# A quarter of a depthwise convolution on GpSimd, and half-array float32 matmuls in turn on both halves of the array

## The chip, the cores and the metric

The kernel runs on one core of one Trainium2 chip. The metric is the time of one execution in microseconds (us), the median of three runs. One execution was profiled; the rows below are from it. The names used are those of the profile: PE is TensorE (matmuls), PEld its weight loads, DVE is VectorE, ACT is ScalarE, POOL is GpSimd, SP is SyncE, which issues most DMAs.

## What is computed

Two model blocks of two layers each, on 256 tokens of width 1024, everything in float32. Two of the token mixers matter here. The first mixer of the first block (the hybrid) contains an attention with a compressed branch: windows of 32 keys (and of 32 values), 15 of them, go through a small network with a gelu. The first mixer of the second block (the even mixer) runs on two streams of 256 tokens (`lat` and `ctx`) and has a convolution branch beside a differential attention.

```
def compress(a, j):                              # hybrid: keys j=0, values j=1
    blocks = a[:, :, blk_idx] + cmp_pe[j]
    h = jax.nn.gelu(blocks.reshape(B, G, n_cmp, CMP_BLOCK * Dh) @ cmp_w1[j])
    return h @ cmp_w2[j]
...
def conformer_conv(p_glu, conv_w, conv_b, ln_g, ln_b):     # even mixer: 512 channels, 31 taps
    a, gate = jnp.split(p_glu, 2, axis=-1)
    u = depthwise_conv(a * jax.nn.sigmoid(gate), conv_w, conv_b)
    return jax.nn.silu(layer_norm(u, ln_g, ln_b))
...
def diff_attend(q, k, v, lam):                   # even mixer
    s = jnp.einsum('bhmqd,bhmkd->bhmqk', q, k).astype(F32) * (DIFF_DQK ** -0.5)
    p = jax.nn.softmax(s, axis=-1)
    p = p[:, :, 0] - lam * p[:, :, 1]
    return jnp.einsum('bhqk,bhkv->bhqv', p.astype(v.dtype), v)
...
    y_lat = jnp.concatenate([conv_lat, diff_merge(o, subln_g, lambda_init)], axis=-1) @ w_out
```

## The kernel before, in words

The kernel is one long program. Each engine executes its own instructions in program order; the order is made by a scheduler from the order of the source and from priorities, so a change in the source can move instructions on an engine. Engines wait for each other by semaphores only.

A projection multiplies the tokens by a weight matrix that streams from memory in tiles of 128x2048 (`wraw`, 1 MB). So that float32 accuracy comes out of a faster matmul form, each half tile (128x1024) is split into a high part `whi` (ACT, L424) and a low part `wlo` (DVE, `wlo = wraw - whi`, L427), and three matmuls replace one (L444 to L446, L506 to L509). Per half tile the DVE thus owes one `wlo`, and PE cannot finish with that half tile before it. The scores, the attention outputs and the compressed branch are plain float32 matmuls; one such matmul stands in the trace as two records.

**The even mixer** (`even_mixer`, from L1889) begins with its projections. The first gives the convolution input, in four groups of 128 channels (j = 0 to 3): `up` holds a group's 2x256 inputs, padded, and `cu[:, j]` its 2x256 outputs. Tap 0 is done on ACT (L1923); each of the other 30 taps is one DVE instruction, `c = u*w + c` over 128x512 (L1933). They are issued in `conv_taps`: all 30 of j = 0, 1 and 2 while the projections run, at a low priority, so that they fill the gaps between the instructions `wlo`. The 30 taps of j = 3 are held in a list and issued in two pieces of 15 after the first and the second attention head. Then come the projections of q and k (`ev_qk`, with a rotation on the DVE, L1943 to L1945) and of v (`ptok`). After the projections follow four attention heads (scores `psc` L1992, row maxima `emx` L1994, softmax, transposes `ppt` L2007, values `poT` L2018). Each head's output is normalised: PE sums squares (`pn`, L617), POOL computes a power of -0.5 (`rir`, L593, 128x4), PE spreads it (`prb`, L629). `conv_norm` takes the channel mean of `cu` (matmul `pmu` L1957) once all taps are done, and has a `rir` of its own. PE fills the gaps of this stage with matmuls for the later adaptive normalisation (`pada` L826), which wait for weights from memory. The output projection ends the mixer.

**The hybrid mixer** (`hybrid`, from L1010) has scores for two groups g of heads, whose keys lie in partitions 0 to 63 (g = 0) and 64 to 127 (g = 1), so each score matmul uses half of the rows of the PE array. The attention outputs (`oT`, L1102) use half of its columns. The compressed branch multiplies 30 rows (2 groups x 15 windows) by `cmp_w1`, 4 tiles of 1 MB that POOL's queue loads: 16 matmuls for j = 0, then 16 for j = 1 (`pc`, L1126), all in the same columns of the array.

Of the kernel before, what the change touches and what calls it, by code (L numbers as in the profile page):

```python
# [8 lines left out]
F32 = mybir.dt.float32  # L9
# [3 lines left out]
OP = mybir.AluOpType  # L13
# [312 lines left out]
TAPJ = (30, 30, 30, 0)  # L326
# [685 lines left out]
def hybrid(S, h, x, gate):  # L1012
    nc, tc, A = S.nc, S.tc, S.A
    mm = nc.tensor.matmul
    with ExitStack() as st:
# [37 lines left out]
        stk = stkb[:, :1024].rearrange("p (j g t) -> p j g t", j=2, g=2)  # L1053
        blk = stkb[:, 1024:1984].rearrange("p (j o g n) -> p j o g n", j=2, o=16, g=2)
        for g in range(2):
            nc.gpsimd.dma_start(stk[0:64, :, g], kk[g * 64:(g + 1) * 64, 0:2])
            nc.gpsimd.dma_start(stk[64:128, :, g, 0:255], kk[g * 64:(g + 1) * 64, 0:2, 1:256])
        pc = S.ps("pc", (128, 2, 256))[:30]
        for j in range(2):
            for g in range(2):  # L1060
                src = bass.AP(tensor=stkb.tensor, offset=stk[:, j, g].offset, ap=[list(stk[:, j, g].ap[0]), [2, 16], [16, 15]])
                nc.vector.tensor_tensor(blk[:, j, :, g], src, pe[:, j * 16:(j + 1) * 16, None].to_broadcast([128, 16, 15]),
                                        op=OP.add)
# [4 lines left out]
        def scores(bi, qt):  # L1068

            kt, n = 2 + bi, 128 * (qt + 1)  # L1070
            sc = big("sc")[:, :8 * n].rearrange("p (i n) -> p i n", i=8)
            for i2 in range(4):
                p = S.ps("psc", (128, 2, 256))
                for a in range(2):
                    i = i2 * 2 + a
                    g, r = i // 4, i % 4
                    b = slice(g * 64, g * 64 + 64)
                    mm(p[:, a, :n], q2[b, r, qt * 128:(qt + 1) * 128], kk[b, kt, :n], start=True, stop=True)
                    nc.vector.scalar_tensor_tensor(sc[:, i], kn(f"d{qt}")[:, :n], slopes[i], p[:, a, :n],
                                                   op0=OP.mult, op1=OP.add)  # L1080
# [24 lines left out]
        def values(bi, qt, sc):  # L1105
            vo = 128 * bi
            for ks in range(qt + 1):
                for g in range(2):
# [18 lines left out]
        u = wk.tile([30, 2, 256], F32, name="gel", tag="e1", bufs=1)  # L1127
        z = wk.tile([30, 2, 256], F32, name="gelz", bufs=1)
        nc.scalar.activation(u, pc, AF.Square)
# [33 lines left out]

        hc = wk.tile([128, 2, 2, 30], F32, name="hc", bufs=1)
        ph = S.ps("phc", (128, 2, 2, 30))
        for j in range(2):
            for hh in range(2):
                nc.tensor.transpose(ph[:, j, hh], z[:, j, hh * 128:(hh + 1) * 128], S.ident[0:30, 0:30])
        nc.vector.tensor_copy(hc, ph)
# [4 lines left out]
        for g in range(2):  # L1174
            for hh in range(2):
                mm(pkc[g * 64:(g + 1) * 64, :15], w2j[:, 0, hh], hc[:, 0, hh, g * 15:(g + 1) * 15], start=hh == 0, stop=hh == 1)
        nc.vector.tensor_copy(kcp[:, :15], pkc[:, :15])
        rep = wk.tile([128, 2, 2, 4, 32], F32, name="rep", bufs=1)
        nc.gpsimd.memset(rep, 0.0)
        for hh in range(2):  # L1180
            for g in range(2):
                nc.vector.tensor_copy(rep[:, hh, g, :, :15], hc[:, 1, hh, None, g * 15:(g + 1) * 15].to_broadcast([128, 4, 15]))
        vcp = []
# [29 lines left out]
        for qt in range(2):  # L1213
            for i in range(8):
                g, r = i // 4, i % 4
# [62 lines left out]
        nc.scalar.activation(pct, pt, AF.Copy)  # L1278
        for g in range(2):
            for r in range(4):  # L1280
                to_o((r, slice(0, 256)), slice(g * 64, g * 64 + 64), vcp[g][:, r], pct[:, g].rearrange("p a b -> p (a b)"))
# [608 lines left out]
def even_mixer(S, hs, xs, gates, neglam, then):  # L1890
# [3 lines left out]
    with ExitStack() as st:  # L1894
# [17 lines left out]
        def ev_conv(f, p):  # L1912
# [66 lines left out]
        def weights_of(hh):  # L1979

            PTs = []
            for i in range(2):
# [3 lines left out]
                for qt in range(2):  # L1986
                    es, rs = [], []
                    for m in range(2):
                        b = slice(m * 64, m * 64 + 64)
                        p = S.ps("psc", (128, nk))  # L1990
                        for a, ks in enumerate(keys):
                            mm(p[:, a * 256:(a + 1) * 256], q[b, hh, i, qt * 128:(qt + 1) * 128], k[b, hh, ks], start=True, stop=True)  # L1992
                        mx = S.sm.tile([128, 1], F32, name=f"emx{m}")
                        nc.vector.tensor_reduce(mx, p, axis=AX, op=OP.max)  # L1994
# [609 lines left out]
```

## Time and profile before

| | |
|---|---|
| median of 3 runs | 2766.69 us (2766.11 to 2767.92) |
| the profiled execution's own time | 2766.61 us |
| its span in the profile | 2764.8 us |
| mean granted TensorE clock | 0.985 of full speed |
| PE busy | 2660.5 us (96%) |
| DVE busy | 1820.6 us (66%) |
| POOL busy | 70.9 us (3%) |

The even mixer's projections and attention lie between about 1585 and 1853 us of the span, the hybrid between 84 and 226 us. The shares of the whole say little on these stretches; the rows further down take them one by one.

### The profile page before, as it was taken

What the parts mean: (1) busy time and instruction counts of PE and PEld (TensorE: products, weight loads), DVE (VectorE), ACT (ScalarE), POOL (GpSimd) and SP (SyncE); (2) the same over time, 40 slices, a digit from 0 to 9 for tenths busy, and PEclk for the clock granted to TensorE, in tenths of its full rate; (3) what the DMA queues carried; (4) which work ended last, traced back from release to release, by engine and by line L of the source; (5) the groups of instructions that cost most, each with busy time, mean ns of one, the idle gap of its engine ahead of it and who ended that gap; (6) DMA issues with size and microseconds to landing.
All of it is one profiled execution on the core that took longest, in us unless ns stands there. A gap on an engine that the chain in (4) does not pass through costs nothing. (4 is left out here: it accounts for less than half of the span.)

```text
span 2764.8 us, 42440 instructions
## 1 busy us (share of the span) xinstructions
PE 2660.5 (96%) x17080; PEld 2135.2 (77%) x17080; DVE 1820.6 (66%) x3010; ACT 1158.5 (42%) x1675; POOL 70.9 (3%) x115
## 2 busy tenths in 40 slices
PE   6999999999899999999999899889999999999999
PEld 2768999879656656555565598489988999799999
DVE  5475888887645555544555487769755467768754
ACT  3354445554644445444444322423222345223543
POOL 0100000000000000000000000000000011000000
PEclk9999999999899999999999999999999999999999
DMA  7645895444799999999999722535555214002552
GB/s 252 226 174 200 339 343 206 181 167 152 295 420 422 413 419 423 404 382 416 408 421 422 319 93 70 205 115 181 197 187 183 92 48 176 30 1 87 205 184 91
DMA packets 92843, 659.95 MB, mean 239 GB/s; under 512 B 10548, under 2 KB 10821, under 8 KB 13982
## 3 DMA queue, kind: packets, MB, share of 16 engines
q1 hardware_dynamic: 89582, 641.62, 59.5%
q0 software_dynamic: 3056, 15.53, 1.6%
q8 instruction: 136, 2.23, 0.3%
q14 instruction: 69, 0.57, 0.1%
HBM read 651.87 MB, written 4.72 MB: 237 GB/s over the span
## 5 line engine op out<-in xcount | busy, mean ns | idle before, releaser
L427 DVE TENSOR_TENSOR wlo<-wraw,whi 128x1024 fp32r<-128x1024 f32 (+1 forms) x683 | 811.0, 1218 | 338.1 <-ACT whi L424 335.3
L424 ACT ACTIVATE whi<-wraw 128x1024 fp32r<-128x1024 f32 (+1 forms) x683 | 705.1, 1054 | 723.4 <-PE oacc L564 182.3
L563 PE MATMUL oacc<-act_h,whi 128*128 128x256 f32 (+1 forms) x720 | 226.9, 316 | 0.0
L564 PE MATMUL oacc<-act_l,whi 128*128 128x256 f32 (+1 forms) x720 | 226.8, 315 | 0.0
L565 PE MATMUL oacc<-act_h,wlo 128*128 128x256 f32 (+1 forms) x720 | 226.8, 315 | 0.0
L792 DVE SCALAR_TENSOR_TENSOR macc<-wraw,srow 128x1024 f32<-128x1024 f32 x144 | 175.9, 1221 | 8.6 <-DMA wraw<-in_ada_dram 4.1
L565 PEld LDWEIGHTS oacc<-act_h,wlo 128*128 128x128 f32 x720 | 135.7, 188 | 10.2
L563 PEld LDWEIGHTS oacc<-act_h,whi 128*128 128x128 f32 x720 | 135.7, 189 | 10.0
L564 PEld LDWEIGHTS oacc<-act_l,whi 128*128 128x128 f32 x720 | 135.6, 188 | 10.0
L507 PE MATMUL pm<-h_lo,whi 128*128 128x256 f32 x512 | 132.7, 280 | 0.0
L506 PE MATMUL pm<-h_hi,whi 128*128 128x256 f32 x512 | 132.1, 278 | 0.0
L427 DVE TENSOR_TENSOR eal<-pat,eah 128x512 fp32r<-128x512 f32 x28 | 19.4, 691 | 167.0 <-ACT eah L424 167.0
L506 PE MATMUL pws<-h_hi,whi 128*128 128x256 f32 x416 | 112.1, 283 | 4.5 <-DVE xg L642 4.5
L1753 PE MATMUL pu<-wraw,gq 128*64 128x512 f32 x448 | 113.4, 595 | 0.0
L507 PE MATMUL pws<-h_lo,whi 128*128 128x256 f32 x416 | 111.4, 282 | 0.0
L1758 ACT ACTIVATE ea<-pg 128x512 f32<-128x512 f32 x42 | 25.1, 597 | 203.8 <-PE pg L1753 162.7
L445 PE MATMUL pyl<-wlo,eah 128*128 128x512 f32 x224 | 90.5, 404 | 18.6 <-DVE wlo L427 17.5
L509 PE MATMUL pm<-h_hi,wlo 128*128 128x256 f32 x512 | 106.8, 279 | 0.0
L444 PE MATMUL pws<-h_hi,whi 128*128 128x256 f32 x352 | 103.5, 294 | 0.0
L1759 DVE TENSOR_TENSOR ea<-ea,pu 128x512 f32<-128x512 f32 x42 | 28.9, 687 | 112.3 <-PE pu L1753 79.6
L1753 PE MATMUL pg<-wraw,gq 128*64 128x512 f32 x448 | 101.3, 595 | 0.0
L446 PE MATMUL pws<-h_hi,wlo 128*128 128x256 f32 x352 | 101.1, 287 | 0.0
(788 smaller groups left out, 6536.0 us busy)
## 6 DMA issues: line engine op xcount, KB each, us to landing
wraw<-in_moe_gu_dram SPq DMA_DIRECT2D x224, 1024.0 KB, 10.0
wraw<-in_moe_down_dram SPq DMA_DIRECT2D x112, 1024.0 KB, 9.6
wraw<-in_mlp_dram SPq DMA_DIRECT2D x64, 1024.0 KB, 4.8
wraw<-in_ada_dram SPq DMA_DIRECT2D x48, 1024.0 KB, 4.8
wraw<-in_dense_gu_dram SPq DMA_DIRECT2D x22, 1024.0 KB, 5.8
wraw<-in_hyb_mod_dram SPq DMA_DIRECT2D x12, 1024.0 KB, 7.1
wraw<-in_dense_mod_dram SPq DMA_DIRECT2D x12, 1024.0 KB, 4.8
wraw<-in_ssm_xbc_dram SPq DMA_DIRECT2D x12, 1024.0 KB, 4.7
```

Of the source, the lines that this page charges most:

```text
L424: self.nc.scalar.activation(hi, src, AF.Copy)
L427: self.nc.vector.tensor_tensor(lo, src, hi, op=OP.subtract)
L444: mm(out, l[0], r[0], start=start, stop=False)
L446: mm(out, l[1], r[0], start=False, stop=stop)
L506: mm(p[:, i], hi[:, k], hs[i][0][:, k], start=st, stop=False, skip_group_check=True)
L507: mm(p[:, i], hi[:, k], hs[i][1][:, k], start=False, stop=False, skip_group_check=True)
L509: mm(p[:, i], lo[:, k], hs[i][0][:, k], start=False, stop=k == 7, skip_group_check=True)
L563: mm(p, wh, h, start=start, stop=False, skip_group_check=True)
L564: mm(p, wh, l, start=False, stop=False, skip_group_check=True)
L565: mm(p, wl, h, start=False, stop=stop, skip_group_check=True)
L792: nc.vector.scalar_tensor_tensor(junk, r[:, j], 1.0, s, op0=OP.mult, op1=OP.mult, accum_out=t[:, f:f + 1])
L1753: mm(pg[gu][q], g[2][:, i, q], w[:, k], start=i == 0, stop=i == 7, skip_group_check=True)
```

## The change

It has two parts, which touch each other nowhere.

The first is in the even mixer. The 30 taps of group j = 3 leave the DVE: POOL does each as two instructions over 128x512, `t = u*w` and `c = c + t`, as soon as that group's `up` and its tap 0 are there, that is during the projections. `t` is a single buffer in SBUF, as are `u` and `c`. The DVE keeps the 90 taps of j = 0 to 2, and the attention stage has no DVE taps any more.

The second concerns matmuls that use half of the array (or fewer columns): in the hybrid's scores, attention outputs and compressed scores and in the even mixer's scores, consecutive matmuls now alternate between the two halves. In the compressed branch, j = 0 and j = 1 go to columns 0 to 31 and 32 to 63 and alternate; the blocks are padded from 30 to 32 columns by a small memset on POOL, the four tiles of `cmp_w1` are loaded in another order (first halves of both j, then second halves), and the gelu runs on 64 partitions x 256 in place of 30 x 512.

```
@@ hybrid
-        blk = stkb[:, 1024:1984].rearrange("p (j o g n) -> p j o g n", j=2, o=16, g=2)
+        blk = stkb[:, 1024:2048].rearrange("p (j o m) -> p j o m", j=2, o=16)
+        nc.gpsimd.memset(blk[:, :, :, 30:32], 0.0)
...
-        pc = S.ps("pc", (128, 2, 256))[:30]
+        pc = S.ps("pc", (128, 256))[:64]
...
-            for i2 in range(4):
-                p = S.ps("psc", (128, 2, 256))
+            for r2 in range(2):
+                ps = [S.ps("psc", (128, 2, 256)) for _ in range(2)]
                 for a in range(2):
...
+                    for g, p in enumerate(ps):
+                        b, r = slice(g * 64, g * 64 + 64), r2 * 2 + a
+                        mm(p[:, a, :n], q2[b, r, qt * 128:(qt + 1) * 128], kk[b, kt, :n], start=True, stop=True)
...
-                    for r in range(4):
+                    both.append(pts)
+                for r in range(4):
+                    for g, pts in enumerate(both):
                         to_o((r, slice(qt * 128, qt * 128 + 128)), slice(g * 64, g * 64 + 64),
...
-        for j in range(2):
-            w1t = [S.raw(A["cmp_w1"][j, :, o * 2048:(o + 1) * 2048], nc.gpsimd).rearrange("p (a b) -> p a b", b=256) for o in range(2)]
-            for o in range(16):
-                mm(pc[:, j], blk[:, j, o].rearrange("p g n -> p (g n)"), w1t[o // 8][:, o % 8], start=o == 0, stop=o == 15)
+        for o2 in range(2):
+            w1t = [S.raw(A["cmp_w1"][j, :, o2 * 2048:(o2 + 1) * 2048], nc.gpsimd).rearrange("p (a b) -> p a b", b=256) for j in range(2)]
+            for o in range(8):
+                for j in range(2):
+                    mm(pc[j * 32:j * 32 + 32], blk[:, j, o2 * 8 + o], w1t[j][:, o], start=o2 + o == 0, stop=o2 + o == 8,
+                       skip_group_check=True)
...
@@ even_mixer
+            if j == 3:
+                t = wk.tile([128, 2, 256], F32, name="tap", bufs=1)
+                for i in range(1, 31):
+                    nc.gpsimd.tensor_scalar(t, u[:, :, i:i + 256], cw[:, j, i:i + 1], None, op0=OP.mult)
+                    nc.gpsimd.tensor_tensor(c, c, t, op=OP.add)
+                return
             for i in range(1, 31):
                 taps.append((c, u[:, :, i:i + 256], cw[:, j, i:i + 1]))
-            conv_taps(TAPJ[j])
+            conv_taps(30)
...
-                    for m in range(2):
-                        b = slice(m * 64, m * 64 + 64)
-                        p = S.ps("psc", (128, nk))
-                        for a, ks in enumerate(keys):
+                    two = [S.ps("psc", (128, nk)) for _ in range(2)]
+                    for a, ks in enumerate(keys):
+                        for m, p in enumerate(two):
+                            b = slice(m * 64, m * 64 + 64)
                             mm(p[:, a * 256:(a + 1) * 256], q[b, hh, i, qt * 128:(qt + 1) * 128], k[b, hh, ks], start=True, stop=True)
...
-            with tc.issue_after(last[TAPA[hh] - 1].ins):
-                conv_taps(TAPB[hh])
```

The diff leaves open where the instructions come to stand. On POOL, in the even mixer before: the last norms ahead of the mixer (`rs`), then at once the five `rir` of the heads and of the convolution, and a DMA issue.

```order
L593 TENSOR_TENSOR rs_21057<-rs1v,mhalf 128x2
L593 TENSOR_TENSOR rs_21064<-rs2v,mhalf 128x2
L593 TENSOR_TENSOR rir<-rirv,mhalf 128x4 x5
L773 DMA srow<-in_conds_dram 128x1024
```

And now, the first rows of the 60 that stand between `rs` and the five `rir` (the other 28 pairs read like these two):

```order
L593 TENSOR_TENSOR rs_21056<-rs1v,mhalf 128x2
L593 TENSOR_TENSOR rs_21063<-rs2v,mhalf 128x2
L1935 ISA
L1935 TENSOR_SCALAR tap<-up,ecw 128x512
L1936 TENSOR_TENSOR cu<-cu,tap 128x512
L1935 TENSOR_SCALAR tap<-up,ecw 128x512
L1936 TENSOR_TENSOR cu<-cu,tap 128x512
```

So all 60 new instructions lie ahead of the first head's `rir` in POOL's queue. On the DVE, at the end of the projections, before (the rows from the last `wlo` of the projections to the first row maximum of the attention):

```order
L427 TENSOR_TENSOR wlo<-wraw,whi 128x1024
L1945 TENSOR_TENSOR k<-k,rt 128x256
L1943 TENSOR_TENSOR rt<-rt,k_rope 128x256
L1944 TENSOR_TENSOR k<-prope,k_rope 128x256
L1933 SCALAR_TENSOR_TENSOR cu<-up,ecw,cu 128x512
L1945 TENSOR_TENSOR k<-k,rt 128x256
L1933 SCALAR_TENSOR_TENSOR cu<-up,ecw,cu 128x512 x11
L1994 TENSOR_REDUCE emx_22336<-psc 128x1
```

And now, from the last `wlo` but one to the same place (L1947 is the tap, L1957 to L1959 the rotation, L2009 the row maximum):

```order
L427 TENSOR_TENSOR wlo<-wraw,whi 128x1024
L1947 SCALAR_TENSOR_TENSOR cu<-up,ecw,cu 128x512 x6
L1957 TENSOR_TENSOR rt<-rt,k_rope 128x256
L1958 TENSOR_TENSOR k<-prope,k_rope 128x256
L1947 SCALAR_TENSOR_TENSOR cu<-up,ecw,cu 128x512
L1959 TENSOR_TENSOR k<-k,rt 128x256
L1957 TENSOR_TENSOR rt<-rt,k_rope 128x256
L1958 TENSOR_TENSOR k<-prope,k_rope 128x256
L1947 SCALAR_TENSOR_TENSOR cu<-up,ecw,cu 128x512
L1959 TENSOR_TENSOR k<-k,rt 128x256
L1947 SCALAR_TENSOR_TENSOR cu<-up,ecw,cu 128x512
L427 TENSOR_TENSOR wlo<-wraw,whi 128x1024
L1947 SCALAR_TENSOR_TENSOR cu<-up,ecw,cu 128x512 x8
L2009 TENSOR_REDUCE emx_22399<-psc 128x1
```

Behind the last `wlo` stood 12 taps and 4 instructions of the rotation; now 8 taps stand there, and all of the rotation lies ahead of it. On PE, in the hybrid, the compressed branch was one run between the projection `pws` and the scores:

```order
L446 MATMUL pws<-h_hi,wlo 128x256
L1126 MATMUL pc<-wraw,stk 30x256 x32
L1078 MATMUL psc<-kk,q_516 128x128 x3
L444 MATMUL ptok<-whi,h_hi 128x256
```

It is now in two runs, with scores (`psc`), transposes (`ptp`) and two other matmuls (`pla`) between them:

```order
L446 MATMUL pws<-h_hi,wlo 128x256
L1134 MATMUL pc<-wraw,stk 32x256 x17
L1078 MATMUL psc<-kk,q_516 128x128 x8
L1115 MATMUL ptp<-kb,sc 128x128 x8
L1160 MATMUL pla<-gk,lr 128x256 x2
L1078 MATMUL psc<-kk,q_516 128x256 x2
L1134 MATMUL pc<-wraw,stk 32x256 x15
L1078 MATMUL psc<-kk,q_516 128x256 x2
```

The matmul count of the branch is the same (32); 17 of them now stand ahead of the other work and 15 behind it.

## Rows read from the trace of the kernel before

**Rows 1.** The page: span, and busy time, share and instructions of each engine.

```profile
span 2764.8 us, 42440 instructions
PE 2660.5 (96%) x17080; PEld 2135.2 (77%) x17080; DVE 1820.6 (66%) x3010; ACT 1158.5 (42%) x1675; POOL 70.9 (3%) x115
```

**Rows 2.** Windows: hybrid; even mixer's projections (second row: j = 3 ready), attention.

```profile
core 0: us, PE busy (x) PEld busy (x) DVE busy (x) ACT busy (x) POOL busy (x), PEclk, DMA share, GB/s
84.00:226.00 142.00, 139.73 (x880) 104.59 (x878) 89.08 (x220) 61.34 (x142) 11.29 (x18) 0.98 0.51 180
...
1645.00:1705.00 60.00, 60.00 (x440) 56.41 (x439) 59.22 (x93) 13.41 (x25) 0.00 (x0) 1.00 0.25 88
1705.00:1714.00 9.00, 9.00 (x41) 7.19 (x39) 0.40 (x1) 1.79 (x3) 0.00 (x0) 1.00 0.00 0
1714.00:1802.00 88.00, 74.00 (x356) 40.94 (x356) 68.29 (x205) 41.78 (x103) 3.80 (x3) 0.90 0.49 179
```

**Rows 3.** Groups of DVE instructions by line and shape, 1645 to 1706 us.

```profile
line engine op names shapes xcount | busy us, mean ns | idle before us <-releasers
L1933 DVE SCALAR_TENSOR_TENSOR cu<-up,ecw,cu 128x512 f32<-128x512 f32 x60 | 42.8, 748 | 0.8
L427 DVE TENSOR_TENSOR wlo<-wraw,whi 128x1024 fp32r<-128x1024 f32 x9 | 11.0, 1218 | 0.0
L1943 DVE TENSOR_TENSOR rt<-rt,k_rope 128x256 f32<-128x256 f32 x8 | 3.3, 418 | 0.0
```

**Rows 4.** DVE timeline around the end of the projections (start, duration, instruction).

```profile
1693.65 1.21 DVE L427 TENSOR_TENSOR wlo<-wraw,whi 128x1024 fp32r<-128x1024 f32 x1
1694.78 0.42 DVE L1945 TENSOR_TENSOR k<-k,rt 128x256 f32<-128x256 f32 x1
1695.12 0.42 DVE L1943 TENSOR_TENSOR rt<-rt,k_rope 128x256 f32<-128x256 f32 x1
...
1696.78 8.62 DVE L1933 SCALAR_TENSOR_TENSOR cu<-up,ecw,cu 128x512 f32<-128x512 f32 x11
1715.31 0.69 DVE L1994 TENSOR_REDUCE emx<-psc 128x1 f32<-128x512 f32 x1 [9.90 <-PE psc L1992]
```

**Rows 5.** Window of the last 24 matmuls of the projections, columns as in rows 2.

```profile
1708.50:1714.10 5.60, 5.60 (x25) 4.32 (x24) 0.00 (x0) 1.79 (x3) 0.00 (x0) 1.00 0.00 0
```

**Rows 6.** POOL timeline: the same 128x4 power alone, then beside DVE.

```profile
1812.34 1.01 POOL L593 TENSOR_TENSOR rir<-rirv,mhalf 128x4 f32<-128x4 f32 x1 [18.76 <-DVE rirv L591]
...
1791.98 0.74 DVE L1933 SCALAR_TENSOR_TENSOR cu<-up,ecw,cu 128x512 f32<-128x512 f32 x1
1792.14 1.45 POOL L593 TENSOR_TENSOR rir<-rirv,mhalf 128x4 f32<-128x4 f32 x1 [20.10 <-DVE rirv L591]
...
209.04 1.22 DVE L427 TENSOR_TENSOR wlo<-wraw,whi 128x1024 fp32r<-128x1024 f32 x1
209.22 1.96 POOL L593 TENSOR_TENSOR rsa<-rsav,mhalf 128x4 f32<-128x4 f32 x1 [83.63 <-DVE rsav L591]
...
2292.58 1.01 POOL L593 TENSOR_TENSOR rl<-rl2v,mhalf 128x4 f32<-128x4 f32 x1
2292.64 0.69 DVE L2222 SCALAR_TENSOR_TENSOR du<-dth,du 128x512 f32<-128x512 f32 x1 [0.63 <-ACT dth L2221]
```

**Rows 7.** POOL timeline: three writes of 128x512 in a row.

```profile
86.25 1.48 POOL L1261 MEMSET S<- 128x512 f32 x3
```

**Rows 8.** The chain that ended last, 1714 to 1802 us: by line, and its end.

```profile
by line: PE pada L826 18.4%; DMA wraw<-in_ada_dram 12.4%; PE psc L1992 12.2%; PE ppt L2007 7.6%; DVE cu L1933 6.5%; PE poT L2018 6.1%; PE prb L629 5.9%; DVE wlo L427 4.9%; POOL rir L593 4.4%; issue 3.3%; PE pn L617 2.3%; DVE emx L1994 2.1%;
...
1751.18 1.19 POOL rir L593
...
1800.90 0.76 DVE cu L1933
1801.71 0.70 PE pmu L1957
```

**Rows 9.** PE timeline: the compressed branch, attention outputs, and matmuls in four column groups against one; scores.

```profile
121.11 14.00 PE L1126 MATMUL pc<-wraw,stk 128*30 128x256 f32 x64
...
145.14 1.58 PE L1102 MATMUL oT<-pts,v 128*64 128x128 f32 x16
...
162.69 1.07 PE L826 MATMUL pada<-wraw,cblk 128*32 128x512 f32 x8
...
189.74 1.04 PE L826 MATMUL pada<-wraw,cblk 128*32 128x512 f32 x2
...
1714.14 2.10 PE L1992 MATMUL psc<-k,q 64*128 64x256 f32 x16
```

**Rows 10.** POOL timeline: the fourth load of the compressed weights; and its queue's median time to landing.

```profile
125.05 0.54 POOL L419 DMA_DIRECT2D wraw<-in_cmp_w_dram  x1 [8.79 <-PE pc L1126]
...
wraw<-in_cmp_w_dram POOLq DMA_DIRECT2D x4, 1024.0 KB, 5.4
```

More of the change, by code (lines that the diff above doesn't have):

```diff
@@ L1061, in hybrid @@
                 src = bass.AP(tensor=stkb.tensor, offset=stk[:, j, g].offset, ap=[list(stk[:, j, g].ap[0]), [2, 16], [16, 15]])
-                nc.vector.tensor_tensor(blk[:, j, :, g], src, pe[:, j * 16:(j + 1) * 16, None].to_broadcast([128, 16, 15]),
+                nc.vector.tensor_tensor(blk[:, j, :, g * 15:g * 15 + 15], src, pe[:, j * 16:(j + 1) * 16, None].to_broadcast([128, 16, 15]),
                                         op=OP.add)
@@ L1071, in scores @@
             sc = big("sc")[:, :8 * n].rearrange("p (i n) -> p i n", i=8)
-            for i2 in range(4):
-                p = S.ps("psc", (128, 2, 256))
+            for r2 in range(2):
+                ps = [S.ps("psc", (128, 2, 256)) for _ in range(2)]
                 for a in range(2):
[L1075 to L1080, printed above, removed]
+                    for g, p in enumerate(ps):
+                        b, r = slice(g * 64, g * 64 + 64), r2 * 2 + a
+                        mm(p[:, a, :n], q2[b, r, qt * 128:(qt + 1) * 128], kk[b, kt, :n], start=True, stop=True)
+                for g, p in enumerate(ps):
+                    for a in range(2):
+                        i = g * 4 + r2 * 2 + a
+                        nc.vector.scalar_tensor_tensor(sc[:, i], kn(f"d{qt}")[:, :n], slopes[i], p[:, a, :n],
+                                                       op0=OP.mult, op1=OP.add)
             m = S.sm.tile([128, 8], F32, name="smax")
@@ L1107, in values @@
             for ks in range(qt + 1):
+                both = []
                 for g in range(2):
@@ L1121, in hybrid @@
         S.proj_ws(h, A["hyb_qk"], lambda f, p: nc.scalar.activation(qk[:, f:f + 2], p, AF.Copy))
-        for j in range(2):
-            w1t = [S.raw(A["cmp_w1"][j, :, o * 2048:(o + 1) * 2048], nc.gpsimd).rearrange("p (a b) -> p a b", b=256) for o in range(2)]
-            for o in range(16):
-                mm(pc[:, j], blk[:, j, o].rearrange("p g n -> p (g n)"), w1t[o // 8][:, o % 8], start=o == 0, stop=o == 15)
-        u = wk.tile([30, 2, 256], F32, name="gel", tag="e1", bufs=1)
-        z = wk.tile([30, 2, 256], F32, name="gelz", bufs=1)
+        for o2 in range(2):
[4 more added lines that the diff above has]
+                       skip_group_check=True)
+        u = wk.tile([64, 256], F32, name="gel", tag="e1", bufs=1)
+        z = wk.tile([64, 256], F32, name="gelz", bufs=1)
         nc.scalar.activation(u, pc, AF.Square)
@@ L1161, in hybrid @@
         S.proj_tok(h, A["hyb_v"], lambda j, tt, p: nc.scalar.activation(v[:, tt], p, AF.Copy))
[L1164 to L1168, printed above, removed]
+        hc = wk.tile([128, 2, 64], F32, name="hc", bufs=1)
+        ph = S.ps("phc", (128, 2, 64))
+        for hh in range(2):
+            nc.tensor.transpose(ph[:, hh], z[:, hh * 128:(hh + 1) * 128], S.ident[0:64, 0:64])
         nc.vector.tensor_copy(hc, ph)
@@ L1175, in hybrid @@
             for hh in range(2):
-                mm(pkc[g * 64:(g + 1) * 64, :15], w2j[:, 0, hh], hc[:, 0, hh, g * 15:(g + 1) * 15], start=hh == 0, stop=hh == 1)
+                mm(pkc[g * 64:(g + 1) * 64, :15], w2j[:, 0, hh], hc[:, hh, g * 15:(g + 1) * 15], start=hh == 0, stop=hh == 1)
         nc.vector.tensor_copy(kcp[:, :15], pkc[:, :15])
@@ L1181, in hybrid @@
             for g in range(2):
-                nc.vector.tensor_copy(rep[:, hh, g, :, :15], hc[:, 1, hh, None, g * 15:(g + 1) * 15].to_broadcast([128, 4, 15]))
+                nc.vector.tensor_copy(rep[:, hh, g, :, :15], hc[:, hh, None, 32 + g * 15:47 + g * 15].to_broadcast([128, 4, 15]))
         vcp = []
@@ L1213, in hybrid @@
         for qt in range(2):
-            for i in range(8):
+            for i in (0, 4, 1, 5, 2, 6, 3, 7):
                 g, r = i // 4, i % 4
@@ L1278, in hybrid @@
         nc.scalar.activation(pct, pt, AF.Copy)
-        for g in range(2):
-            for r in range(4):
+        for r in range(4):
+            for g in range(2):
                 to_o((r, slice(0, 256)), slice(g * 64, g * 64 + 64), vcp[g][:, r], pct[:, g].rearrange("p a b -> p (a b)"))
@@ L1987, in weights_of @@
                     es, rs = [], []
-                    for m in range(2):
-                        b = slice(m * 64, m * 64 + 64)
-                        p = S.ps("psc", (128, nk))
-                        for a, ks in enumerate(keys):
+                    two = [S.ps("psc", (128, nk)) for _ in range(2)]
+                    for a, ks in enumerate(keys):
+                        for m, p in enumerate(two):
+                            b = slice(m * 64, m * 64 + 64)
                             mm(p[:, a * 256:(a + 1) * 256], q[b, hh, i, qt * 128:(qt + 1) * 128], k[b, hh, ks], start=True, stop=True)
+                    for m, p in enumerate(two):
                         mx = S.sm.tile([128, 1], F32, name=f"emx{m}")
```

## The prediction

> **What bounds the kernel now.** I read the page first. PE is busy 96% of the span, DVE 66%, POOL 3% [rows 1]. That looks as if DVE work were free to move and POOL were idle. It holds as an average only, so I read each touched stretch by windows.
>
> The hybrid (84 to 226 us) is bound by PE: 139.73 of 142 us busy [rows 2]. PE time saved there should leave the total. In the even mixer's projections, from 1645 us (when the input of j = 3 is ready) to 1705, **two engines are full at once**: PE 60.00 of 60 us, DVE 59.22 of 60 [rows 2]. PE is fed by `wlo`, which stands among taps and rotation on an in-order DVE. The groups by line show 93 DVE instructions there, of which 60 are taps (42.8 us) and 9 are `wlo` (11.0 us) [rows 3]. All but the four rotation instructions with a PSUM input read two tensors from SBUF. How much delay the DVE can bear is read from the timeline: the last `wlo` ends at 1693.65 + 1.21 = 1694.9 us [rows 4], and the matmuls that need it (the last 24) run from 1708.5 [rows 5]. It is 13.6 us ahead. After it DVE has taps left until 1705.4, then waits 9.90 us for the scores [rows 4]. In the attention (1714 to 1802) no engine is full: PE 74.0 of 88, DVE 68.3 [rows 2]. The chain of waits there spends 18.4% on `pada`, 12.4% on its DMA, 6.5% on taps, and it ends through a last run of taps into `pmu` [rows 8].
>
> **The change, part by part.**
>
> *Taps off the DVE.* 30 taps leave the attention. A tap is 748 ns [rows 3], so 22 us of DVE work go, but the chain holds only 6.5% of 88 us = 5.7 us of them [rows 8]. I take -6 us. Bounds: 0, if something else is then last ahead of `pmu`, and -10, if the chain's `wlo` (4.9%, 4.3 us [rows 8]) was late because of taps too.
>
> *Taps on POOL.* 60 POOL instructions of 512 elements a partition start at about 1646 us, in the stretch where DVE has no free time. No POOL instruction of that shape that reads is in the trace. What POOL does beside DVE is: the power of 128x4 takes 1.01 us alone, 1.45 us when a tap had started 0.16 us before it, 1.96 us when a `wlo` had started 0.18 us before it [rows 6]. In both cases it ends a constant time after the DVE instruction does: 1793.59 against 1792.72 (0.87 us), 211.18 against 210.26 (0.92 us). So POOL's read waited until the DVE instruction let go. The other direction is bare: a power that began 0.06 us ahead of a two-input DVE instruction left it at 0.69 us [rows 6], but it reads four elements. One side waiting for the other is the sign of a shared path, and I take it that DVE waits in turn while POOL reads 512 elements.
>
> [...]
>
> How long is a hold? POOL writes 128x512 three times in 1.48 us, and one write alone is 0.54, so a pass over 512 elements is (1.48 - 0.54)/2 = 0.47 us [rows 7]. The multiplication reads one tensor (one pass), the addition two (two passes): 3 x 0.47 = 1.41 us per tap, 42 us for 30 taps. Lower bound 0: DVE is never held. Upper bound: POOL holds the path for its whole instruction; the fixed part of one, by the powers' delay behind the DVE instruction, is up to 0.4 us more, 60 x 0.39 + 42 = 65 us. Nearest to a 512-element read is the pass, so I take 42.
>
> [...]
>
> Of this hold DVE has slack for a part. In the new order 4 taps and 4 rotation instructions more lie ahead of the last `wlo`: 4 x 0.79 (start to start in the run of 11 [rows 4]) + 4 x 0.34 = 4.5 us. Slack: 13.6 - 4.5 = 9.1 us. If all 60 POOL instructions get their turn ahead of the last `wlo` (84 or so DVE instructions lie before it), PE finishes the projections 42 - 9 = **33 us** later. If POOL gets only every second gap, some 42 of the 60 lie ahead: 30 - 9 = 21 us, and the other 12 us of hold fall into the attention, where DVE has 20 us free. So 21 to 33; I take 33, since a 0.4 us fixed part fits into one 0.75 us tap.
>
> POOL's queue: the five `rir` are behind all 60. The first is wanted at 1751 [rows 8]. POOL alone would need 30 x (1.41 + 0.8) = 66 us; waiting once per instruction for a tap's remainder (0.4 us) makes it 90, so the end is at 1736 us: the `rir` is not late, by 15 us here and by 48 in the forecast, where the attention itself starts later.
>
> *Compressed branch.* `pc` is 64 records in 14.00 us, one set of columns [rows 9]. That columns work side by side is seen on `pada`: eight records over four column groups take 1.07 us, two over one 1.04 [rows 9]. Pairing halves 14.0: -7.0 us. But the fourth weight tile waits for the slot of the first: it was issued at 125.05, with 5.4 us to landing [rows 10], so 130.5 us. The first 17 matmuls end at about 121.1 + 17 x 0.22 = 124.8; the work placed behind them (psc x8, ptp x8, pla x2, psc x2, about 3.9 us) reaches to 128.7. PE then waits 1.8 us. Net -5.2.
>
> *Other half-array matmuls.* The even mixer's scores overlap already: 16 records take 2.10 us, where 216 ns a record (as in `pc`) would make 3.5 [rows 9], as the halves alternate every two matmuls. Little is left, and DVE and DMA pace that stage: 0. `oT` in the hybrid takes 1.58 us for 16 records [rows 9], serially 1.75 and paired 0.88, so up to 0.7 us per run; with some runs overlapped already I take -2 for all of these. The hybrid is -7 in sum; bounds 0 (overlapped, and the fourth tile's wait takes the rest) and -15 (all such runs halved). Memset, gelu and transposes, under 1 us each, lie beside PE's projections; without that cover they cost 1 us.
>
> **Sum.** The profiled execution's own time is 2766.61 us, its median 2766.69, 0.1 apart; the span is 1.8 less. 2766.6 + 33 - 6 - 7 = **2787 us**.
>
> **The rivals.**
>
> *Only POOL gives way (faster).* Each POOL read waits for the DVE's instruction, DVE is never held. Place: the projections. For it: in every row POOL is the one that waits [rows 6]; against it: those reads are too short to show a hold. Price: the 33 us vanish, 2766.6 - 6 - 7 = 2753.6; with the bounds of the two gains 2742 to 2761. It decides when DVE's hold is below 9 + 13 = 22 us, that is 0.37 us per POOL instruction. Chance 0.24.
>
> *A short hold.* DVE is held for one pass per POOL instruction or less, 22 to 30 us in sum: 13 - 21 us of delay against 13 of gain, 2766 to 2775 us; with gains at their bounds 2760 to 2775. Chance 0.10.
>
> *A long hold.* 65 us, the upper bound: 2766.6 + 56 - 13 = 2810 us, above my range. Chance 0.07.
>
> *The half-array part does nothing.* The pairs overlap already, and the fourth tile's wait returns what `pc` saves: 7 us less gain in each case, 2794 us for the forecast. For it: the 2.10 us of `psc` [rows 9]; against it: `pc` at 216 ns a record. It shifts the cases and changes no sign. Chance 0.2, inside the others.
>
> **How the numbers follow.** The forecast (hold of 30 to 50 us, delay 21 to 41) has 0.59: 2775 to 2800, its own range. Two runs of this kernel tell from no change at about 0.2%, 5.5 us: 2761 to 2772. Faster: the first rival but for its upper edge (0.22), and 0.02 of the short hold, 0.24. Same: 0.02 + 0.06 = 0.08. Slower: the rest, 0.59 + 0.07 + 0.02 = 0.68. The range 2750 to 2800 leaves out the long hold, some of the first rival's lower edge and the forecast's upper edge, 0.17 in sum.
>
> **What would show it.** Right: from 1646 us on, L1947 taps and `wlo` with means well above 748 and 1218 ns, or gaps between them, in step with POOL; PE with idle time before `ptok` released by `wlo`; the last `wlo` at about 1730 us or later; no L1947 in the attention; `pc` in two runs of 3.7 and 3.3 us with a gap of 1 to 3 us ahead of the second. Wrong: DVE taps at 748 ns with POOL's instructions stretched between them (the first rival), or POOL ending so late that the first `rir` and its `prb` wait for it, which would put the loss into the attention.

## The result, and the profile after

The changed kernel takes 2783.64 us (median of 5 runs, 2779.92 to 2785.95) against 2766.69 us before: a ratio of 1.0060, 95% interval 1.0049 to 1.0071. That is slower by 17 us, where 2787 was forecast. Single runs of before lie between 2760 and 2776 us over all these runs, so differences of a few us are read from ratios with their intervals, or from stretches of the traces that repeat from run to run.

The page of the changed kernel (answers to [rows 1]); its own time was 2782.06 us:

```profile
span 2780.3 us, 42475 instructions
PE 2661.5 (96%) x17078; PEld 2130.8 (77%) x17078; DVE 1838.9 (66%) x2980; ACT 1159.3 (42%) x1675; POOL 175.2 (6%) x176
```

DVE has 30 instructions fewer and yet 18 us more busy time. Windows over the hybrid, the projections and the attention (answers to [rows 2]; the mixer begins 6.7 us earlier here):

```profile
core 0: us, PE busy (x) PEld busy (x) DVE busy (x) ACT busy (x) POOL busy (x), PEclk, DMA share, GB/s
84.00:226.00 142.00, 135.74 (x927) 103.53 (x926) 90.69 (x223) 64.22 (x147) 9.66 (x16) 0.98 0.54 195
...
1645.00:1705.00 60.00, 49.26 (x348) 45.88 (x347) 59.82 (x62) 11.70 (x21) 57.09 (x33) 0.91 0.16 53
...
1727.20:1817.20 90.00, 77.08 (x346) 38.09 (x346) 56.32 (x175) 42.09 (x103) 22.99 (x16) 0.85 0.46 161
```

In the same 60 us DVE finishes 62 instructions in place of 93, though it is as busy; PE falls from 60.0 to 49.3 us and its granted clock from 1.00 to 0.91. (The mixer stands some 7 us earlier in this window; e2 below, which is as early and has no taps on POOL, finishes 85 DVE instructions in it with PE at 60.0 us.) DVE's groups show which instructions grew (answers to [rows 3]):

```profile
line engine op names shapes xcount | busy us, mean ns | idle before us <-releasers
L1947 DVE SCALAR_TENSOR_TENSOR cu<-up,ecw,cu 128x512 f32<-128x512 f32 x37 | 42.7, 1195 | 0.2
L427 DVE TENSOR_TENSOR wlo<-wraw,whi 128x1024 fp32r<-128x1024 f32 x7 | 11.8, 1680 | 0.0
```

A tap went from 748 to 1195 ns in the mean, a `wlo` from 1218 to 1680. The timeline of both engines shows one POOL instruction at a time doing it (L1936 is POOL's addition, L1935 its multiplication; undisturbed, L1947 takes 0.75 us, L427 1.22, L1957 to L1959 0.42):

```profile
1654.12 1.89 POOL L1935 TENSOR_SCALAR tap<-up,ecw 128x512 f32<-128x512 f32 x1
1654.49 1.18 DVE L1947 SCALAR_TENSOR_TENSOR cu<-up,ecw,cu 128x512 f32<-128x512 f32 x1
...
1656.09 1.30 POOL L1936 TENSOR_TENSOR cu<-cu,tap 128x512 f32<-128x512 f32 x1
1656.27 2.20 DVE L427 TENSOR_TENSOR wlo<-wraw,whi 128x1024 fp32r<-128x1024 f32 x1
1657.49 2.67 POOL L1935 TENSOR_SCALAR tap<-up,ecw 128x512 f32<-128x512 f32 x1
...
1658.73 0.83 DVE L1957 TENSOR_TENSOR rt<-rt,k_rope 128x256 f32<-128x256 f32 x1
...
1660.24 1.44 POOL L1936 TENSOR_TENSOR cu<-cu,tap 128x512 f32<-128x512 f32 x1
1660.47 1.49 DVE L1959 TENSOR_TENSOR q<-q,rt 128x256 f32<-128x256 f32 x1
```

An addition adds 0.98 us to a `wlo` and 1.07 to a rotation; a multiplication adds 0.43 to a tap and 0.41 to a rotation. And the wait works both ways: the multiplication that starts at 1657.49 behind the stretched `wlo` takes 2.67 us. POOL alone, in the attention, is faster:

```profile
1731.72 1.56 POOL L1935 TENSOR_SCALAR tap<-up,ecw 128x512 f32<-128x512 f32 x1
1733.37 1.26 POOL L1936 TENSOR_TENSOR cu<-cu,tap 128x512 f32<-128x512 f32 x1
1734.73 1.56 POOL L1935 TENSOR_SCALAR tap<-up,ecw 128x512 f32<-128x512 f32 x1
```

The end of the projections (answers to [rows 4]):

```profile
1718.81 1.21 DVE L427 TENSOR_TENSOR wlo<-wraw,whi 128x1024 fp32r<-128x1024 f32 x1
1719.95 10.00 DVE L1947 SCALAR_TENSOR_TENSOR cu<-up,ecw,cu 128x512 f32<-128x512 f32 x8
1729.87 1.28 DVE L2009 TENSOR_REDUCE emx<-psc 128x1 f32<-128x512 f32 x2
```

The last `wlo` ends at 1720.0 us, which is 82.8 us after the input `up` of j = 3 began; before, it was 50.9 us after it. Before, PE came to the first matmul that needs it 13.9 us after it was done (1694.9 us, [rows 4]):

```profile
1708.78 0.39 PE L445 MATMUL ptok<-wlo,h_hi 128*128 128x512 f32 x1
```

Now PE waits 3.4 us for it, and the scores follow 7.1 us later (5.4 before):

```profile
1716.24 0.40 PE L444 MATMUL ptok<-whi,h_hi 128*128 128x512 f32 x1
1720.08 0.50 PE L445 MATMUL ptok<-wlo,h_hi 128*128 128x512 f32 x1 [3.44 <-DVE wlo L427]
...
1727.17 2.00 PE L2006 MATMUL psc<-k,q 64*128 64x256 f32 x16
```

What PE waited for from 1600 to 1745 us (in total, times, longest; the wait in `psc` is in the attention):

```profile
PE prope L1956 <- ACT rt L1953: 10.6, 3, 6.6
PE psc L2006 <- ACT e L2013: 4.2, 1, 4.2
PE ptok L445 <- DVE wlo L427: 3.4, 1, 3.4
...
```

The greater part is not `wlo`, but the wait for the last `wlo` is the one that ends the projections. `prope` is the rotation's matmul; it waits for ACT's copy `rt`, which waits until the DVE's rotation has let go of one of two buffers.

The table sets the traces side by side. The stretches are the differences of starts in each trace: P from the input `up` of j = 3 to the first scores `psc`; A from there to the mean `mu` of `conv_norm`; H from the first copy of the hybrid's keys to the first of the last four splits of its output (`mix_l`). Ratios are to runs of before on the same chip; the one run of before beside the four single ones took 2771.00 us.

| kernel | ratio, 95% interval | P, us | A, us | H, us |
|---|---|---|---|---|
| before | | 70.2 | 88.7 | 136.0 |
| changed | 1.0060 (1.0049 to 1.0071) | 89.9 | 90.1 | 130.0 |
| e1, taps on POOL only | 1.0046 (1.0032 to 1.0060) | 88.3 | 85.4 | 132.7 |
| e2, half-array part only | 1.0001 (0.9988 to 1.0014) | 70.2 | 93.0 | 128.8 |
| e3, no taps of j = 3 | 0.9953 (0.9932 to 0.9973) | 70.2 | 86.9 | 130.2 |
| e4, POOL writes only | 0.9959 (0.9943 to 0.9975) | 70.2 | 87.0 | 129.0 |
| e5, POOL multiplies only | one run, 2768.66 | 72.5 | 85.0 | 134.3 |
| e6, j = 2 into the attention | 1.0056 (1.0034 to 1.0077) | 80.1 | 93.7 | 130.4 |
| e7, compressed branch only | one run, 2778.66 | 70.2 | 91.7 | 139.4 |
| e8, even scores only | 1.0019 (1.0008 to 1.0029) | 70.2 | 92.6 | 132.5 |
| e9, hybrid part only | 1.0005 (0.9992 to 1.0018) | 70.2 | 93.2 | 130.4 |
| e10, four rt buffers | one run, 2781.96 | 91.2 | 84.6 | 130.1 |
| e11, e6 with four rt buffers | one run, 2779.16 | 71.2 | 97.2 | 134.0 |
| e12, 12 taps into DVE's wait | 0.9968 (0.9955 to 0.9980) | 70.2 | 82.1 | 136.9 |

P is the steady one: without POOL's reads it is 70.15 to 70.20 us in eight kernels. A and H vary by 3 to 5 us in kernels whose code there is the same (before, e7 and e9 have one attention: 88.7, 91.7, 93.2). The granted clock differs there too (0.90, 0.86, 0.87 over A) and explains only part of it.

### The profile page after: what moved, and what is told of

It reads as the page before. It is cut to its first block, busy times and chain, and to the rows that moved or that the text cites. A ratio compares the mean times of both kernels' runs of the same rounds, so it can differ in the third digit from the quotient of the medians.

```text
span 2780.3 us, 42475 instructions
## 1 busy us (share of the span) xinstructions
PE 2661.5 (96%) x17078; PEld 2130.8 (77%) x17078; DVE 1838.9 (66%) x2980; ACT 1159.3 (42%) x1675; POOL 175.2 (6%) x176
## 5 line engine op out<-in xcount | busy, mean ns | idle before, releaser
L427 DVE TENSOR_TENSOR wlo<-wraw,whi 128x1024 fp32r<-128x1024 f32 (+1 forms) x683 | 814.9, 1223 | 325.4 <-ACT whi L424 322.5
L507 PE MATMUL pm<-h_lo,whi 128*128 128x256 f32 x512 | 132.7, 280 | 0.0
L427 DVE TENSOR_TENSOR eal<-pat,eah 128x512 fp32r<-128x512 f32 x28 | 19.4, 691 | 167.0 <-ACT eah L424 167.0
```

The source lines that it names most:

```text
L427: self.nc.vector.tensor_tensor(lo, src, hi, op=OP.subtract)
L507: mm(p[:, i], hi[:, k], hs[i][1][:, k], start=False, stop=False, skip_group_check=True)
```

## The experiments

**Which part is it?** e1 is before with the first part of the change alone (the diff's lines in `even_mixer` on j = 3 and `conv_taps`), e2 before with the second alone.

> The convolution part alone; all matmuls as before. [...] In the changed kernel the attention began 13.0 us late after an even mixer that began 6.7 us early, so the part alone should cost 15.4 + 7.2 = 22.6 us: 2789 us (2786 to 2792). Rival (the parts need each other: it is the earlier start or the new order of the scores that collides with the taps): 2767 to 2780 us.

Measured: 2779.02 us (10 runs), +12.7 us, less than expected; but P is 88.3 us. The cost in the projections is there without the other part, so the parts need not meet for it; the total of 2779.0 lies in the rival's range all the same. What was wrong was to take the 7.2 us of earliness as the hybrid's gain: H is 132.7 us here with the hybrid untouched, and the 136.0 of before has a stretch at a lower clock (6.8 us at 0.50).

> The half-array part alone; all 120 taps on the DVE as before. Theory: the 7.2 us by which the changed kernel was early from the end of the hybrid on stays to the end: 2759.5 us (2758 to 2762). Rival (the new order of the even mixer's scores costs in the attention, whose length rose by 1.3 us in the changed kernel): 2762 to 2766 us, with the attention 90 us or longer.

Measured: 2768.48 us (10 runs), no gain, which is outside both ranges; A is 93.0 us, as long as the rival had it. The earliness is in the trace (H 128.8) and is gone at the end.

**What of POOL holds the DVE?** e3 and e4 keep the second part and the DVE's 90 taps; e3 drops the tile and the loop below as well.

```
@@ changed kernel -> e3 (no POOL instruction), e4 (four writes a tap)
             if j == 3:
                 t = wk.tile([128, 2, 256], F32, name="tap", bufs=1)
                 for i in range(1, 31):
-                    nc.gpsimd.tensor_scalar(t, u[:, :, i:i + 256], cw[:, j, i:i + 1], None, op0=OP.mult)
-                    nc.gpsimd.tensor_tensor(c, c, t, op=OP.add)
+                    nc.gpsimd.memset(t, 0.0)        # e4 only, and three more
```

> The changed kernel with the 30 taps of j = 3 left out altogether, on POOL and on DVE, so that group keeps tap 0 only. Theory (hold): no tap or wlo is stretched, the attention begins 6 to 7 us ahead of before, at about 1707.5 us of the span. If DVE's freed 22 us shorten the attention by the 6 us that were forecast, the total is 2753 us; if DVE taps were not what the attention waited for, 2759 to 2760 us. Rival (the loss comes from the order of the DVE's instructions or from PE's clock, not from POOL): 2770 us or more.

Measured: 2755.33 us (5 runs), by the ratio 13 us less than before (7 to 19). P is 70.2: without POOL's instructions nothing is lost there.

> The changed kernel with each pair of POOL instructions replaced by four memsets of 128x512 (120 in all, some 60 us of POOL writes and no reads); the 30 taps of j = 3 are left out. Theory (reads hold): DVE taps stay at 0.75 us and wlo at 1.22 us, the total is that of the kernel without these taps within 3 us (2753 to 2763 us). Rival (any POOL instruction on SBUF holds the DVE): taps of more than 1 us beside the memsets, 0.47 us each or some 56 us in sum, 2780 us or more.

Measured: 2757.73 us (6 runs). The groups of the DVE from 1610 to 1656 us, while POOL wrote 128x512 all the time (it had nothing to wait for, and its writes ran from 1582.7 to 1656.8), and POOL's:

```profile
L1949 DVE SCALAR_TENSOR_TENSOR cu<-up,ecw,cu 128x512 f32<-128x512 f32 x46 | 31.5, 742 | 0.1
L427 DVE TENSOR_TENSOR wlo<-wraw,whi 128x1024 fp32r<-128x1024 f32 x9 | 10.9, 1217 | 0.2 <-ACT whi L424 0.2
```

```profile
L1935 POOL MEMSET tap<- x30: 515/526/541, 1582.7 to 1655.0; 128x512 f32 x30
L1936 POOL MEMSET tap<- x30: 524/526/543, 1583.7 to 1655.6; 128x512 f32 x30
```

Neither side stretches the other (742 and 1217 ns beside 748 and 1218 undisturbed). It is the reads. In this kernel all of the rotation and all but 6 taps stand ahead of the last `wlo`, more than in the changed one, and P is 70.2: the order by itself costs nothing.

e5 leaves out the line with the addition.

> The changed kernel with POOL's 30 multiplications alone; the additions into cu are left out, so j = 3 keeps tap 0 only. Theory (a POOL instruction holds the DVE while it reads, one pass of 512 elements for one input, two for two): taps beside a multiplication are stretched by 0.3 to 0.45 us, 10 to 13 us in sum, none by 1.0, and the stretch from the input of j = 3 to the first scores is 70 to 75 us. Rival (a GpSimd instruction with one SBUF input does not hold the DVE, the hold is the additions' alone): all taps at 0.75 us and 70.2 us.

Measured: P 72.5 us. DVE's groups from 1645 to 1706 us:

```profile
L1946 DVE SCALAR_TENSOR_TENSOR cu<-up,ecw,cu 128x512 f32<-128x512 f32 x49 | 43.9, 935 | 0.4
L427 DVE TENSOR_TENSOR wlo<-wraw,whi 128x1024 fp32r<-128x1024 f32 x8 | 10.6, 1319 | 0.0
```

49 x (935 - 748) = 9.2 us and 8 x (1319 - 1218) = 0.8, 10 us in these two groups, and POOL's 30 multiplications all start in this stretch (1645.9 to 1702.7 us): one-input instructions hold too, by some 0.33 us each, where the theory had 0.3 to 0.45.

**Is DVE's time what is short?** e6 gives the DVE 30 taps less to do in the projections.

```
@@ changed kernel -> e6
-TAPJ = (30, 30, 30, 0)
+TAPJ = (30, 30, 0, 0)
-            conv_taps(30)
+            conv_taps(TAPJ[j])
...
             S.tick(3)
+            with tc.issue_after(last[TAPA[hh] - 1].ins):
+                conv_taps(TAPB[hh])
```

> The changed kernel, but the DVE's 30 taps of j = 2 are moved out of the projections into the attention, in the two pieces in which those of j = 3 were; POOL still does j = 3 beside the projections. Theory (the loss is DVE time in the projections): DVE has 22 us less of its own to do there and 30 to 43 us of hold, so the last wlo is late by less than its slack of 9 to 14 us and the attention begins within 3 us of its place in the kernel with the half-array part alone (1708 us): total 2766 to 2772 us. Rival (POOL's taps are the loss wherever DVE's lie, by a late last tap, a late rir or the clock): 2778 us or more.

Measured: 2779.56 us (4 runs), a miss: P is 80.1. The last `wlo` was early (1699.5 us), and PE still lost 8.1 us in `prope`. So the rival was open again, and e10 and e11 put the buffers to the test, in the changed kernel and in e6.

```
@@ changed kernel -> e10, e6 -> e11
-            t = wk.tile([128, 256], F32, name="rt")
+            t = wk.tile([128, 256], F32, name="rt", bufs=4)
...
-                t = wk.tile([128, 2, 256], F32, name="tap", bufs=1)
+                t = wk.tile([128, 2, 256], F32, name="tap", tag="mixt")
```

> The changed kernel with four buffers in place of two for rt, the rotation's copy (and the tap buffer laid into another tile's place, to make room). From the input of j = 3 to the first scores of the attention the kernel takes 70.2 us before and 89.9 us with the change, 19.8 more; in the trace PE waits 10.6 of them in prope for ACT's rt, which waits for the DVE's rotation to let go of a buffer, and 3.4 for the last wlo. Theory (DVE's time is what is short: 27 us of hold and 4.5 us of moved instructions ahead of the last wlo, against 13.6 of slack): the waits in prope go and come back as waits for wlo, the stretch stays within 87 to 90 us. Rival (the loss is the rotation's two buffers, which stop PE): the stretch falls by the 10 us, to 78 to 81 us.

Measured: P 91.2 us, a little above the theory's range, and all of PE's waiting in the projections is now for `wlo`:

```profile
PE ptok L445 <- DVE wlo L427: 12.8, 3, 6.2
```

> The same four buffers of rt in the kernel where the DVE's taps of j = 2 lie in the attention; that kernel took 80.1 us for the stretch, with the last wlo early (done at 1699.5 us) and 8.1 us of PE waits in prope. Theory: there DVE has time enough and only the rotation's buffers hold PE up, so the stretch is 70 to 73 us, that of before. Rival (POOL's reads cost PE's stretch 10 us in another way, as by the clock): 78 us or more.

Measured: P 71.2 us, with 0.8 us left for `wlo`:

```profile
PE psc L2006 <- ACT e L2013: 2.7, 1, 2.7
PE ppt L2022 <- DVE e L2019: 0.9, 1, 0.9
PE ptok L445 <- DVE wlo L427: 0.8, 1, 0.8
```

The four kernels form a square. With DVE overfull, more buffers only move PE's wait from `prope` to `wlo` (89.9, 91.2). The last `wlo` is done 82.8 us after `up` in the changed kernel, in e1 and in e10 alike, and P differs between them only by what PE takes from the first matmul that needs it to the scores: 7.1, 5.5 and 8.3 us, at a granted clock of 0.76, 1.00 and 0.63 (in the changed kernel 3.4 us of it at 0.50), after waits of 3.4, 1.6 and 6.2 us for that `wlo`. With DVE relieved, the buffers are the one obstacle left, and without it P is that of before within 1 us (80.1, 71.2). e11 is no better in all, since its attention has the DVE's taps and the end of POOL's.

**Where did the half-array gain go?** e9 takes only the diff's lines in `hybrid`, e8 only those on the scores in `weights_of`.

> The half-array part in the hybrid mixer alone (scores, values, compressed branch and compressed scores); even mixer as before. Theory: the hybrid's matmuls save 3 to 4 us, since of the 7.2 us by which the changed kernel was early some 3 to 5 appear too where the hybrid is untouched; this stays to the end: 2762 to 2764 us. Rival (the gain is 7 us, and it was lost again in the even mixer of the kernel that had the half-array part alone): 2759 us.

Measured: 2766.64 us (12 runs). A gain of over 2.2 us is outside the interval.

> Only the new order of the even mixer's scores (both halves in turn, both row maxima after all of them); all else as before. Theory: the halves overlapped already, and the first row maximum now waits for the second half's scores as well, 16 times; this costs 2 to 6 us in the attention and is where the hybrid's gain went: 2769 to 2772 us. Rival (the order does nothing, and the hybrid's gain was only a matter of single executions): 2766 to 2767 us.

Measured: 2771.80 us (12 runs), 2 to 8 us slower by the interval. The attention of its one trace (92.6 us) does not differ from e9's with the old order (93.2), so neither the place of this loss nor its cause was found; and e2, which has both parts, would by e8 and e9 be at 1.0024 and was at 1.0001.

e7 is before with the lines on `blk`, `pc`, `cmp_w1`, the gelu and `hc`.

> Only the compressed branch in pairs (with its loads, gelu and transposes), all else as before. The stretch from the first copy of the hybrid's keys to its last output copy takes 132.6 us with the hybrid untouched (two kernels; 136.0 in the trace of before, which has a stretch at a lower clock) and 129.8 us in the mean of six kernels with the whole half-array part. Theory: pairing pc saves 5 us of PE there, but PE then waits for the fourth weight tile and for wlo, and of the 2.8 us that are left most is pc's: 130 to 131 us. Rival (the 2.8 us are the scores' and attention outputs'): 132 to 133 us.

Measured: H 139.4 us, inconclusive, since its matmuls there ran at a lower clock for a while (the second run of `pc` took 5.33 us, in the changed kernel 3.64). An estimate settles it in part: 13.6 us of this stretch ran at a granted clock of 0.5, and half of them taken off leaves 132.6 us, the value of the rival. The same estimate takes the 136.0 of before to 132.6, where e1 and e8, at full clock throughout, measured 132.7 and 132.5. So `pc` alone seems to save nothing there.

**A better version.** e3 shows that the attention is shorter without DVE taps, and [rows 4] that DVE waits 9.90 us ahead of it. e12 is before with 12 taps of j = 3 moved there.

```
@@ before -> e12
-TAPJ = (30, 30, 30, 0)
+TAPJ = (30, 30, 30, 12)
```

> The kernel before, with 12 of the 30 taps of j = 3 issued behind the last wlo of the projections, where the DVE waits 9.9 us for the first scores, and 18 in the attention as before; POOL has none. Theory: 12 x 0.787 = 9.4 us fit into that wait, the stretch from the input of j = 3 to the first scores stays at 70.2 us, and the attention, which was 6 us shorter without the 30 taps (87 against 93 us in the traces), gives back 12/30 of it: 2 to 3 us less than before in the total, a ratio of about 0.999. Rival (only the taps at the attention's end are on the path, or DVE's wait is needed for something): within 1 us of before, or up to 3 us slower if the first row maximum is late.

Measured: 2759.96 us (6 runs), 5.5 to 12.5 us faster than before, which is the fastest version here that computes all. DVE's timeline at the end of the projections (the row of taps holds the last 15 of 20 behind the last `wlo`, where 12 stood before; the other 4 of the 12 went ahead of it):

```profile
1699.88 11.39 DVE L1933 SCALAR_TENSOR_TENSOR cu<-up,ecw,cu 128x512 f32<-128x512 f32 x15
1714.60 0.69 DVE L1994 TENSOR_REDUCE emx<-psc 128x1 f32<-128x512 f32 x1 [3.33 <-PE psc L1992]
```

The wait for the scores shrank from 9.90 to 3.33 us and P stayed. The gain is over twice the 12/30 of 6 us that was expected. The traces show a reason. In before, the attention's taps are the last thing that the mean `mu` waits for: the last starts at 1800.9 us, `mu` at 1802.9. In e12 the last tap stands 21 us ahead of it (first and last start):

```profile
L1933 DVE SCALAR_TENSOR_TENSOR cu<-up,ecw,cu x120: 731/750/753, 1616.2 to 1774.7; 128x512 f32<-128x512 f32 x120
L1959 DVE TENSOR_SCALAR mu<-pmu x1: 683/683/683, 1795.6 to 1795.6; 128x512 f32<-128x512 f32 x1
```

So in this one trace of e12 (A 82.1 us) the 18 taps that stay are off the end of the stage as well, and the gain need not be in proportion to the taps moved.

## Why the prediction was right, and where it was off

*DVE is held while POOL reads: right, and rightly sized.* Forecast 0.47 us per input and instruction, 1.41 per tap; measured on single instructions 0.41 to 0.43 for the multiplication and 0.98 to 1.07 for the addition. In sum it is a little less. These are the DVE's two main groups from POOL's first tap to the start of the last `wlo`:

```profile
L1947 DVE SCALAR_TENSOR_TENSOR cu<-up,ecw,cu 128x512 f32<-128x512 f32 x52 | 58.9, 1171 | 0.4
L427 DVE TENSOR_TENSOR wlo<-wraw,whi 128x1024 fp32r<-128x1024 f32 x8 | 13.0, 1624 | 0.0
```

52 x (1171 - 748) + 8 x (1624 - 1218) is 25.2 us, and the rotation adds 2.5: some 28 us beside 43 POOL instructions, 0.65 each or 1.3 per tap. Reads hold (a tap takes 935 ns in e5) and writes do not (742 ns in e4). In the rotation the two instructions with both inputs in SBUF took up to 830 (L1957) and 1505 ns (L1959); L1958, whose other input lies in PSUM, took 409 to 414 ns in all its eight instances. The hold is shorter than the POOL instruction, most of all for the multiplication: 0.98 to 1.07 of 1.26 us for the addition, 0.4 of 1.56 us for the multiplication.

*How much of it counts: the mis-sized term.* The step "42 - 9 = 33" took all 60 POOL instructions to lie ahead of the last `wlo`. Only 43 had been done by then, 21 taps and one multiplication, since a POOL tap alone takes 3.0 us (1731.72 to 1734.73) and not the 2.2 that were worked out, and beside DVE 3.2 to 4.6. Their hold of 28 us and the 8 DVE instructions that moved ahead (some 4 us) make the last `wlo` 31.9 us later. Of this 13.9 us were slack, so PE's first matmul that needs it is 18.0 us later, and what follows to the scores takes 1.7 us more at a lower clock (0.76 against 1.00): 19.8 in all, the rise of P. So where 33 was forecast, 19.8 was measured. The variant with every second gap, 42 of 60 instructions and 21 us, came nearest, though POOL's own time per tap is reason enough for the 43.

*What PE waits for: the right place, but not the only one.* The prediction looked for PE waiting in `ptok` for `wlo`, and that wait ends the projections; 10.6 of PE's 14.0 us of waiting come earlier, in `prope`, which it did not foresee. e10 shows that this is the same shortage seen earlier in PE's queue, not a second cost: without it PE waits 12.8 us for `wlo` and P is no shorter. Nor did the prediction give the clock a term: behind the last `wlo` it costs 1.7 us here, 0.1 in e1 and 3.0 in e10.

*The attention, -6 us: right in size.* A is 91.8 us in the mean of the five kernels with DVE taps and no POOL (before, e2, e7, e8, e9) and 86.3 in the three without either in that stage (e3, e4, e5). In the changed kernel, e1 and e10, where POOL still works into it, the mean is 86.7. With the new order of the scores on both sides it is 92.8 (e2, e8) against 86.3. The single pair of traces hides this (88.7 and 90.1).

*The hybrid, -7 us: near in the stage itself, and gone at the end.* `pc` did run in pairs and did wait for the fourth tile, for 2.41 us where 1.8 were worked out:

```profile
118.08 4.07 PE L1134 MATMUL pc<-wraw,stk 128*32 128x256 f32 x34
122.09 1.99 PE L1078 MATMUL psc<-kk,q 64*128 64x128 f32 x16
...
129.21 3.64 PE L1134 MATMUL pc<-wraw,stk 128*32 128x256 f32 x30 [2.41 <-DMA wraw<-in_cmp_w_dram]
```

That is 7.71 us in place of 14.00; the scores fell from 12.95 (e1) to 9.31 us and the attention outputs from 13.00 to 11.34, together more than the 2 that were forecast. But PE's idle time in the hybrid rose from 2.3 to 6.3 us, and waits for `wlo` there (2.8 us) are new: a stage that is PE-bound at 139.7 of 142 us need not stay so once PE is faster. H is 130.8 us in the mean of nine kernels with this part and 134.5 in four without. With half of the time at a clock of 0.5 taken off, as for e7, the nine have 125.5 to 127.3 and the four 131.8 to 132.7, some 6 us by this estimate; but all nine have such a stretch, and two of the four. Nothing of it is sure to reach the end (e9). Over the experts' stage (from their routing to the first `up` of the even mixer) seven of those nine traces take 932.8 to 933.1 us, and the four without the part 930.4 to 930.7 (the changed kernel 931.0). All of this difference arises in the last 31 us, at the branch behind the experts and just after it: there PE waits 1.3 to 2.2 us for ACT's sequencer in the seven and 0.3 to 0.5 in the four. Why is open.

*The even scores: taken at 0, +5 in e8.* e2, which has them too, does not show it, so this term is not settled.

*The sum: near, and partly by luck.* The taps alone cost 12.7 us (e1) where 33 - 6 = 27 was forecast, and the half-array part gave nothing (e2) where 7 was: two errors of opposite sign, the second of which hid half of the first. The 4 us between 12.7 + 0 and the measured 17 are not placed; the intervals of e1 and of the changed kernel overlap.

Some of the prediction's side figures do not follow from its own bounds. With gains of 0 to 25 us the first rival reaches up to 2767 us, not 2761, and the short hold spans 2755 to 2788, not 2760 to 2775. Eight, not four, of the rotation's instructions in [rows 3] have a PSUM input. The forecast's sum does not change by this.

The rival in which only POOL gives way falls with e1 and e5. The short hold falls with the rows of 0.98 us, though the 28 us of hold that counted lie in its 22 to 30. That the half-array part brings nothing was given 2 in 10, and is what e2 shows.

## What to carry to other kernels

Before work goes to an idle engine, ask what it shares with the busy one: here each tap that POOL took over saved the DVE 0.75 us and blocked it for about 1.3, so it could not pay where the DVE had no free time. Look for the wait inside the busy engine's own queue first; here the 9.9 us that DVE waited at a stage's border were worth more than a second engine. And where an in-order engine is starved, the wait shows at whatever is next in its queue (10.6 us in `prope`, with four buffers 12.8 in `ptok`): relieve one cause at a time and see whether the wait moves or goes, and ask which wait ends last, not which is longest in sum: here 3.4 us for the last `wlo` decided, and 10.6 us ahead of it did not.

## What the runs showed of the hardware that was not expected

That each side waits for the other was expected; how far POOL is drawn out was not. By tile, in the changed kernel (duration in ns: least, median, most; first and last start):

```profile
L1935 POOL TENSOR_SCALAR tap<-up,ecw x30: 1565/1887/2968, 1638.1 to 1744.1; 128x512 f32<-128x512 f32 x30
L1936 POOL TENSOR_TENSOR cu<-cu,tap x30: 1262/1395/1865, 1641.2 to 1745.9; 128x512 f32<-128x512 f32 x30
```

```profile
L1947 DVE SCALAR_TENSOR_TENSOR cu<-up,ecw,cu x90: 737/755/1789, 1610.2 to 1728.9; 128x512 f32<-128x512 f32 x90
```

POOL's multiplication was drawn out by up to 1.4 us and a DVE tap by up to 1.05. The hold lies inside the instruction: the DVE's taps and `wlo` grew to 1171 and 1624 ns in the mean with 0.4 and 0.0 us of idle time ahead of them, so engines held each other here by more than the semaphores that the description of the kernel before allows for. The multiplication is also the slower of POOL's two (1.56 against 1.26 us alone), though it reads half as much. And kernels with the same attention code took 88.7 to 93.2 us for it in single traces, so such a stage can't be compared by one trace each.
